# Encoder block on one core: the first tile of x in two transfers, and the root's spread in two rounded passes

## The chip, the cores and the metric

One core of a Trainium2 chip runs the kernel. The metric is the device time of one execution in microseconds (us), taken as the median of several runs. The core has five engines that work side by side: TensorE (PE, matrix products), VectorE (DVE), ScalarE (ACT), GpSimd (POOL) and SyncE (SP, which issues the transfers here). Each runs its own list of instructions in order, and they wait for each other through semaphores.

## The reference

One layer of a bidirectional encoder, batch 1, 1024 tokens, width 1024, all in float32:

```
h = rmsnorm(x, norm1_g)
q, k, v, u = split(h @ w_in)                 # 512, 128, 128, 512 columns
a = attention_mixer(q, k, v, ...)            # 8 query heads, 2 key heads, 2-D rotary positions
p = pool_mixer(u, ...)                       # 4 groups of 128 channels, windows 2/4/8/16
x = x + concat([a, p]) @ w_out
h = rmsnorm(x, norm2_g)
x = x + (silu(h @ w_gate) * (h @ w_up)) @ w_down
```

`rmsnorm` multiplies each token's row by r = 1/sqrt(mean of squares + 1e-6) and by a gain per channel.

## The kernel before

**Products.** Every float32 product is made from rounded (F32R) operands. `split` (L336 to L349) writes an operand's rounded copy, the high half, and then the rest, the low half (`combine`, L351 to L355: source minus high half). Three matmuls, high by high, high by low and low by high (`PASSES`, L324), give one product; matmuls of the feed-forward part are L1176, L1441 and L1494, those of the first projections L490 (k and v), L684 (u) and L601 (q).

**Start.** `load_x` (L434) fetches x in eight tiles of 128 tokens into `qp`; tile 0 goes first, then k's and v's weights (`load_w`, L415, two transfers of 512 KB), then tiles 1 to 7, all on SP's queue. `turn_x` (L458) transposes a tile, eight PE transposes of 128x128 (L474); ACT writes each one's high half (L464) and DVE its low half (L466). `stats_x` (L447) makes r for each token (`rx`, one column for each tile) with an iterated root on DVE (L362 to L373).

**Spread of r.** The u projection is held transposed (channels on partitions), so r, which belongs to a token, has to stand along the free axis, the same on all partitions. `diagonals` (L648) writes for each tile the identity times its column of r (L655, a 128x128 piece of the 1024 wide tile `dgs`); `spread_r` (L660) multiplies a tile of ones by it (L665), which sums each column and so puts r on every partition; ACT copies it out (L669). Two such products with 512 columns each are made, in full float32, just after the first step of the first group of u (`K["spread"]`).

**Who decides the order.** The whole program is written once into a planner, `Flow` (L139): every piece of ACT, DVE and POOL work is a job whose steps have a cost by the functions `act`, `dve`, `pool` and so on (L264 to L286), PE's work advances the planner's clock by the number in `flow.tensor(...)`, transfers by `Flow.load`. Where a step may run on either of two engines (`quicker`, L252, used by `split` and `combine`), the planner takes the one that it expects to end first. The program is rehearsed six times, jobs get ranks from when PE needed them, and the best rehearsal's order is what the engines run. So a changed cost near the start can move low halves between DVE and POOL, and change each engine's order, anywhere behind it. PE's order and SP's are as written.

**Later stages.** After u come the pooling windows (`windows`, L714) with their product (`pool_mix`, L752, matmul L760), the q projection (`q_tile`, L595), attention (L828 scores, L858 transposes of probabilities, L871 values, L908 output), and a feed-forward part of blocks (L1176) and, five times, `down_sums` (L1469), which multiplies sums of operands (steps A11, S1, S2, S4, S3, A12 and A22, each for two operand pairs; L1494) and adds their banks to x by DVE (`into`, L1456). In `down_sums` the two operands of a step are split into a `ring` tile and a `raw` or `wk` tile, high halves by ACT (L340), low halves by DVE or POOL (L355).

Of the kernel before, what the change touches and what calls it, by code (L numbers as in the profile page):

```python
# [10 lines left out]
F32 = mybir.dt.float32  # L11
F32R = mybir.dt.float32r
BF16 = mybir.dt.bfloat16
I32 = mybir.dt.int32
AF = mybir.ActivationFunctionType
ALU = mybir.AluOpType
AX = mybir.AxisListType.X

P = 128
# [14 lines left out]
HALF = S // 2  # L34
# [10 lines left out]
NRAW = 3  # L45
RIM, GAP = 120, 80
K = {
    "pieces": 1, "groups": [[0], [1], [2, 3], [4, 5, 6, 7]], "take": [0, 3], "tables": 2, "spread": [1],
    "ahead": [22, 39], "turn_k": 50, "wq": [60], "mix": [56, 62, 10, 30], "prep_q": [20], "turn_q": [37],
    "wo": [33, 39, 52, 62], "score": [40, 41, 42, 43, 47, 49, 52, 54, 57, 59, 61, 63, 63], "fold": 1,  # L50
    "out": [0, 0, 0, 2, 1, 2, 1, 2], "wo2": [3, 9, 10, 10, 16, 16], "mix_c": 5, "norm": 6, "next_prep": 8,
# [212 lines left out]
def act(n, extra=0.0):  # L264
    return "A", 0.1 + 0.00097 * n + extra


def dve(n):

    return "D", max(0.16, 0.07 + 0.00119 * n)  # L270


def dve_sbuf(n):
    return *dve(n), True
# [15 lines left out]
def block_kernel(  # L290
# [4 lines left out]
    nc = tc.nc  # L295
# [17 lines left out]
    ident = const.tile([P, P], F32, name="ident")  # L313
# [11 lines left out]
    flow = Flow(ranks)  # L325
# [65 lines left out]
    def work(dt=F32, n=D):  # L391
        return wk.tile([P, n], dt, tag="wk", name="wk")
# [50 lines left out]
    rx = const.tile([P, NT], F32, name="rx")  # L443
# [202 lines left out]
    rb, rb_jobs, dg_jobs = [], [], []  # L646

    def diagonals():  # L648
        dgs, ones = work(), work(n=P)
        nc.gpsimd.memset(ones, 1.0)  # L650

        def diagonal(t):
            yield [rx_job[t]]
            yield dve_sbuf(P)
            nc.vector.tensor_scalar(dgs[:, t * P:(t + 1) * P], ident, rx[:, t:t + 1], None, op0=ALU.mult)  # L655

        dg_jobs.extend(flow.add(diagonal(t)) for t in range(NT))
        return dgs, ones

    def spread_r(dgs, ones):  # L660
        rb.append(work())
        for h in range(2):
            pr = bank()
            flow.tensor(0.86, *dg_jobs[4 * h:4 * h + 4])
            nc.tensor.matmul(pr, ones, dgs[:, h * HALF:(h + 1) * HALF], start=True, stop=True)  # L665

            def evacuate(h, pr):
                yield act(HALF)
                nc.scalar.activation(rb[0][:, h * HALF:(h + 1) * HALF], pr, AF.Copy)  # L669

            rb_jobs.append(flow.add(evacuate(h, pr)))
            flow.hold("b1", rb_jobs[-1])
# [850 lines left out]
    groups = K["groups"]  # L1523
# [13 lines left out]
    kf.append(flow.add(k_finish(4, 4)))  # L1537
    pw, pw_job = load_pw()
    dgs, ones = diagonals()
    wq = []  # L1540
    step = 0
# [167 lines left out]
```

## Time and profile before

| | us |
|---|---|
| median of 3 runs | 1088.13 (1088.09 to 1088.22) |
| the profiled execution | 1088.39 |
| its span | 1086.5 |
| PE busy | 1064.8 |
| DVE busy | 738.7 |
| ACT busy | 511.1 |
| POOL busy | 461.9 |

The span runs from the first to the last instruction that the profile shows; 1.89 us of the profiled execution lie outside it. The profiled execution is 0.26 us above the median of the runs. An engine's busy time is what its instructions took, waiting left out. PE is busy for 98% of the span, so the time is the time that its matmuls take, plus the stretches in which it waits.

### The profile page before, as it was taken

To read this page: it belongs to the slowest core of one execution; us is meant where nothing else is said; L and a number is where in the kernel's file an instruction comes from. 1 tells how busy PE (TensorE), PEld (TensorE's weight loads), DVE (VectorE), ACT (ScalarE), POOL (GpSimd) and SP (SyncE) were. 2 spreads that over 40 slices of the span, in tenths; PEclk is the share of its full clock that TensorE was granted. 3 is DMA by queue.
4 is the path that set the end of the run, shared out by engine and by line. 5 is a ranking of instruction groups with operands and counts; after the bars stand their busy time and mean duration, and the time that the engine had idled before them with its cause. 6 is when DMAs were issued, how large, how long until landed. Compare 5 with 4: busy or idle time off the path is not lost.

```text
span 1086.5 us, 13908 instructions
## 1 busy us (share of the span) xinstructions
PE 1064.8 (98%) x5114; PEld 875.4 (81%) x5114; DVE 738.7 (68%) x1214; ACT 511.1 (47%) x904; POOL 461.9 (43%) x367
## 2 busy tenths in 40 slices
PE   7999998999999999999999999999999999999998
PEld 6887876888888888878788887888788878888787
DVE  7888788888676766784964379346944496448745
ACT  6424477666676664633433433433333433343340
POOL 1254344444323223444543465355634463446431
PEclk9999999999999999999999999999999999999999
DMA  7122111000000100130032101220213013110114
GB/s 258 30 78 78 39 41 48 10 21 20 10 21 11 30 30 26 53 110 26 20 97 79 39 20 59 78 78 1 78 59 97 2 39 97 59 40 20 40 58 155
DMA packets 42563, 58.47 MB, mean 54 GB/s; under 512 B 4224, under 2 KB 32768, under 8 KB 42496
## 3 DMA queue, kind: packets, MB, share of 16 engines
q1 hardware_dynamic: 42496, 57.59, 16.5%
q8 instruction: 40, 0.66, 0.3%
q14 instruction: 27, 0.22, 0.1%
HBM read 53.39 MB, written 4.19 MB: 53 GB/s over the span
## 4 chain that ended last, share of the span: by engine, by line
PE 78%; DVE 13%; issue 3%; POOL 3%; ACT 2%; DMA 0%; SPq 0%; ACTq 0%; POOLq 0%; DVEq 0%
PE b L1176 36%; PE b L908 8%; PE b L1494 8%; PE b L871 5%; PE b L828 5%; PE b L858 5%; PE b L684 4%; DVE wk L355 3%; PE b L601 3%; DVE ring L355 2%; PE b L1441 2%; POOL wk L355 2%; DVE qp L1456 2%; PE b L490 2%; DVE nm L837 1%
## 5 line engine op out<-in xcount | busy, mean ns | idle before, releaser
L1176 PE MATMUL b<-wk,ring 128*128 128x512 f32 x1872 | 426.3, 390 | 0.9 <-POOL ring L355 0.7
L1176 PEld LDWEIGHTS b<-wk,ring 128*128 128x128 f32 x1872 | 351.1, 188 | 74.6 <-POOL ring L355 1.1
L340 ACT ACTIVATE ring<-raw 128x512 fp32r<-128x512 f32 x130 | 81.6, 629 | 119.6 <-PE b L1176 57.1
L355 POOL TENSOR_TENSOR ring<-raw,ring 128x512 fp32r<-128x512 f32 x54 | 70.1, 1297 | 157.9 <-ACT ring L340 139.1
L847 POOL TENSOR_SCALAR wk<-wk,rsm 128x1024 f32<-128x1024 f32 x64 | 73.6, 1158 | 132.7 <-ACT wk L839 40.2
L349 DVE TENSOR_TENSOR wk<-b,wk 128x512 fp32r<-128x512 f32 (+1 forms) x160 | 101.7, 658 | 41.4 <-ACT wk L340 40.9
L340 ACT ACTIVATE wk<-b 128x512 fp32r<-128x512 f32 (+1 forms) x160 | 90.3, 576 | 84.0 <-PE b L858 67.1
L1494 PE MATMUL b<-raw,ring 128*128 128x512 f32 x480 | 115.3, 394 | 4.1 <-DVE raw L355 2.5
L1494 PEld LDWEIGHTS b<-raw,ring 128*128 128x128 f32 x480 | 88.6, 188 | 29.2 <-DVE qp L1456 5.9
L355 DVE TENSOR_TENSOR ring<-raw,ring 128x512 fp32r<-128x512 f32 x76 | 57.8, 761 | 76.9 <-ACT ring L340 76.9
L1456 DVE TENSOR_TENSOR qp<-qp,b 128x512 f32<-128x512 f32 (+1 forms) x157 | 101.8, 674 | 9.0 <-PE b L1441 8.9
L908 PE MATMUL b<-wk 128*128 128x512 f32 x384 | 102.5, 397 | 0.0
L355 POOL TENSOR_TENSOR wk<-wk 128x512 f32<-128x512 f32 (+3 forms) x52 | 75.9, 1467 | 35.0 <-ACT wk L340 25.8
L828 PE MATMUL b<-kT,wk 128*128 128x512 f32 x256 | 89.5, 431 | 0.5 <-ACT wk L804 0.5
L871 PE MATMUL b<-wk,vv 128*128 128x512 f32 x256 | 83.1, 400 | 4.3 <-DVE wk L349 4.2
L1494 PE MATMUL b<-wk,ring 128*128 128x512 f32 x360 | 85.0, 392 | 0.2
L837 DVE TENSOR_REDUCE nm<-b 128x1 f32<-128x1024 f32 x64 | 77.9, 1217 | 9.1 <-PE b L828 7.9
L908 PEld LDWEIGHTS b<-wk 128*128 128x128 f32 x384 | 70.7, 188 | 14.9
L355 POOL TENSOR_TENSOR ring<-silu,ring 128x512 fp32r<-128x512 f32 x35 | 53.9, 1540 | 63.4 <-ACT ring L340 63.4
L1494 PEld LDWEIGHTS b<-wk,ring 128*128 128x128 f32 x360 | 67.2, 188 | 16.4 <-DVE ring L355 1.8
L858 PEld LDWEIGHTS b<-ident,wk 128*128 128x128 f32 x512 | 63.6, 140 | 16.9 <-POOL wk L847 0.5
L858 PE MATMUL b<-ident,wk 128*128 128x128 f32 x512 | 76.7, 272 | 0.3 <-POOL wk L847 0.3
(142 smaller groups left out, 1454.1 us busy)
## 6 DMA issues: line engine op xcount, KB each, us to landing
raw<-in_w_gate_dram SPq DMA_DIRECT2D x22, 512.0 KB, 3.7
raw<-in_w_up_dram SPq DMA_DIRECT2D x22, 512.0 KB, 3.8
wk<-in_w_down_dram SPq DMA_DIRECT2D x20, 512.0 KB, 4.7
raw<-in_w_in_dram SPq DMA_DIRECT2D x10, 512.0 KB, 4.2
qp<-in_x_dram SPq DMA_DIRECT2D x8, 512.0 KB, 8.2
raw<-in_w_out_dram SPq DMA_DIRECT2D x8, 512.0 KB, 3.4
out_dram<-qp SPq DMA_DIRECT2D x15, 256.0 KB, 2.0
raw<-in_x_dram SPq DMA_DIRECT2D x14, 256.0 KB, 2.7
```

What stands on the lines that cost most here:

```text
L340: nc.scalar.activation(hi, src, AF.Copy)
L349: nc.vector.tensor_tensor(lo, src, hi.bitcast(F32), op=ALU.subtract)
L355: (nc.gpsimd if way[0] == "G" else nc.vector).tensor_tensor(dst, a, b, op=op)
L828: nc.tensor.matmul(s[:, c * 512:(c + 1) * 512], qT[t][0][:, h * P:(h + 1) * P], kT[:, kv, b, c * 512:(c + 1) * 512], start=(b == 0), stop= ...
L837: nc.vector.tensor_reduce(nm, s, axis=AX, op=ALU.max, negate=True)
L847: nc.gpsimd.tensor_scalar(pe, pe, rs, 1.0, op0=ALU.mult, op1=ALU.mult)
L858: nc.tensor.transpose(pt[:, j * P:(j + 1) * P], pe[:, c * P:(c + 1) * P], ident)
L871: nc.tensor.matmul(po[t, kv], vt, ps[:, b], start=(c == 0 and b == 0), stop=(c == NT - 1 and b == 1))
L908: nc.tensor.matmul(self.py, mix[self.t][a][:, k, :], wo[k][b][:, self.cs], start=(self.i == 0 and i == 0), stop=(self.i == NK - 1 and i == 2))
L1176: nc.tensor.matmul(bank_, w[0][:, a, i], x[:, b], start=(start and i == 0 and j == 0), stop=(stop and i == PARTS - 1 and j == 2), skip_gro ...
L1456: nc.vector.tensor_tensor(dst, dst, src, op=op)
L1494: nc.tensor.matmul(banks[t][0], x[:, a, t * P:(t + 1) * P], y[:, b], start=(own == name and i == 0 and j == 0), stop=(i == 1 and j == 2), ...
```

## The change

`K["pieces"]` goes from 1 to 2: tile 0 of x (512 KB) is fetched as two transfers of 128x512 (256 KB each), so that its first four transposes need the first one only; the other tiles are fetched as before. The spread of r gets its diagonals as rounded pairs: ACT writes the high half (identity times r, rounded), DVE the rest, and each 512-column product is made of two F32R matmuls that add up in the bank, in place of a full float32 one. `ones` is written by POOL from the identity in place of a memset, and one more work tile is held.

```diff
 K = {
-    "pieces": 1, "groups": [[0], [1], [2, 3], [4, 5, 6, 7]], "take": [0, 3], "tables": 2, "spread": [1],
+    "pieces": 2, "groups": [[0], [1], [2, 3], [4, 5, 6, 7]], "take": [0, 3], "tables": 2, "spread": [1],
@@
     def diagonals():
-        dgs, ones = work(), work(n=P)
-        nc.gpsimd.memset(ones, 1.0)
+        dgs, ones = [work(F32R) for _ in range(2)], work(F32R, n=P)
+        nc.gpsimd.tensor_scalar(ones, ident, 0.0, 1.0, op0=ALU.mult, op1=ALU.add)
 
         def diagonal(t):
+            c = slice(t * P, (t + 1) * P)
             yield [rx_job[t]]
+            yield act(P)
+            nc.scalar.activation(dgs[0][:, c], ident, AF.Copy, scale=rx[:, t:t + 1])
             yield dve_sbuf(P)
-            nc.vector.tensor_scalar(dgs[:, t * P:(t + 1) * P], ident, rx[:, t:t + 1], None, op0=ALU.mult)
+            nc.vector.scalar_tensor_tensor(dgs[1][:, c], ident, rx[:, t:t + 1], dgs[0][:, c].bitcast(F32), op0=ALU.mult, op1=ALU.subtract)
@@
-            flow.tensor(0.86, *dg_jobs[4 * h:4 * h + 4])
-            nc.tensor.matmul(pr, ones, dgs[:, h * HALF:(h + 1) * HALF], start=True, stop=True)
+            flow.tensor(0.462, *dg_jobs[4 * h:4 * h + 4])
+            for i in range(2):
+                nc.tensor.matmul(pr, ones, dgs[i][:, h * HALF:(h + 1) * HALF], start=(i == 0), stop=(i == 1))
```

Lines behind the change stand 4 further down in the changed kernel (L1456 becomes L1460).

**What moves.** PE's list differs only in the spread, SP's only in the first tile of x. The lists of DVE, POOL and ACT come out of the planner anew, and differ in many places. Three are shown; a name with a number is one tile, and numbers differ between the kernels throughout.

POOL, low halves during the windows and the q weights, before:

```order
L355 TENSOR_TENSOR wk_1053<-wk_945,wk_1052 128x1024
L355 TENSOR_TENSOR wk_1089<-raw_1086,wk_1088 128x1024
L704 MEMSET le_1118 128x8
L706 COPY le_1118<-wk_951 128x16
L711 TENSOR_TENSOR le_1119<-le_1118 128x23
L355 TENSOR_TENSOR wk_1163<-wk_959,wk_1162 128x1024
```

and of the change:

```order
L355 TENSOR_TENSOR wk_1063<-wk_895,wk_1062 128x1024
L355 TENSOR_TENSOR wk_1103<-raw_1100,wk_1102 128x1024
L355 TENSOR_TENSOR wk_1107<-raw_1104,wk_1106 128x1024
L708 MEMSET le_1134 128x8
L710 COPY le_1134<-wk_965 128x16
L715 TENSOR_TENSOR le_1135<-le_1134 128x23
```

The rows that read a `raw` tile are low halves of q's weights, the third and, now, the fourth transfer of them too. The last row of before, the low half of the pooled values of the third group (source wk_959), is no longer POOL's: DVE makes it, in place of the low half of the fourth transfer.

DVE, in the first `down_sums`, around its step S3, before:

```order
L355 TENSOR_TENSOR wk_4986<-wk_4986 128x512
L355 TENSOR_TENSOR ring_5363<-wk_4535,ring_5363 128x512
L355 TENSOR_TENSOR ring_5384<-silu_4611,ring_5384 128x512
L1456 TENSOR_TENSOR qp_84<-qp_84,b1_5255 128x512
L1456 TENSOR_TENSOR qp_84<-qp_84,b3_5260 128x512
L355 TENSOR_TENSOR silu_4980<-silu_4981,silu_4982 128x512
L1456 TENSOR_TENSOR qp_84<-qp_84,b3_5266 128x512
L355 TENSOR_TENSOR wk_5031<-wk_5031 128x512
L1456 TENSOR_TENSOR qp_84<-qp_84,b3_5273 128x512
L355 TENSOR_TENSOR ring_5426<-silu_4646,ring_5426 128x512
L355 TENSOR_TENSOR raw_5406<-wk_5031,raw_5406 128x512
L355 TENSOR_TENSOR wk_5427<-wk_4988,wk_5427 128x512
```

and of the change:

```order
L355 TENSOR_TENSOR ring_5374<-wk_4547,ring_5374 128x512
L355 TENSOR_TENSOR wk_4999<-wk_4999 128x512
L355 TENSOR_TENSOR ring_5395<-silu_4623,ring_5395 128x512
L1460 TENSOR_TENSOR qp_84<-qp_84,b1_5267 128x512
L1460 TENSOR_TENSOR qp_84<-qp_84,b1_5272 128x512
L355 TENSOR_TENSOR silu_4993<-silu_4994,silu_4995 128x512
L1460 TENSOR_TENSOR qp_84<-qp_84,b1_5278 128x512
L355 TENSOR_TENSOR wk_5041<-wk_5041 128x512
L1460 TENSOR_TENSOR qp_84<-qp_84,b3_5285 128x512
L355 TENSOR_TENSOR raw_5416<-wk_5041,raw_5416 128x512
L355 TENSOR_TENSOR ring_5437<-silu_4658,ring_5437 128x512
L355 TENSOR_TENSOR wk_5438<-wk_5001,wk_5438 128x512
```

Two things changed places: the weight sum (wk_4986, now wk_4999) goes from before the two `ring` low halves to between them, and the `raw` low half goes ahead of the `ring` one behind the four `into` additions. The same stands in all five `down_sums`.

DVE at the start (L466: low halves of tile 0's transposes, 128x128; L342 and L355: halves of k's and v's weights), before:

```order
L466 SCALAR_TENSOR_TENSOR wk_114<-b2_150,pk_72,wk_106 128x128
L342 CAST wk_130<-raw_128 128x256
L466 SCALAR_TENSOR_TENSOR wk_114<-b1_147,pk_72,wk_106 128x128
L342 CAST wk_130<-raw_128 128x256
L355 TENSOR_TENSOR wk_131<-raw_128,wk_130 128x256
```

and of the change:

```order
L466 SCALAR_TENSOR_TENSOR wk_114<-b2_151,pk_72,wk_106 128x128
L466 SCALAR_TENSOR_TENSOR wk_114<-b1_148,pk_72,wk_106 128x128
L466 SCALAR_TENSOR_TENSOR wk_115<-b1_154,pk_72,wk_107 128x128
L342 CAST wk_131<-raw_129 128x256 x2
L466 SCALAR_TENSOR_TENSOR wk_115<-b2_161,pk_72,wk_107 128x128
```

Two more of tile 0's low halves stand ahead of the first copy of the weights.

## Rows read from the trace of the kernel before

**Rows 1.** The page, part 1: busy us (share of the span) xinstructions.

```profile
PE 1064.8 (98%) x5114; PEld 875.4 (81%) x5114; DVE 738.7 (68%) x1214; ACT 511.1 (47%) x904; POOL 461.9 (43%) x367
```

**Rows 2.** Busy time by stretch: us, then PE, PEld, DVE, ACT, POOL busy, PEclk, DMA share, GB/s.

```profile
105.00:250.00 145.00, 139.61 (x730) 112.96 (x729) 116.03 (x212) 95.29 (x162) 65.79 (x53) 1.00 0.09 30
250.00:1086.00 836.00, 828.16 (x3846) 679.75 (x3843) 535.23 (x783) 367.34 (x644) 360.42 (x270) 1.00 0.16 50
```

**Rows 3.** Chain of work that ended last, the start: start us, us, what.

```profile
1.16 3.88 DMA qp<-in_x_dram
...
7.05 0.20 DVE wk L342
...
8.87 0.52 DVE wk L466 x2
```

**Rows 4.** Timeline of SP and PE, the start: start us, us, engine, line, operation [idle before <-releaser].

```profile
1.16 0.42 SPq L438 DMA_DIRECT2D qp<-in_x_dram  x1
...
9.32 0.98 PE L490 MATMUL b<-wk 128*128 128x256 f32 x3
...
12.54 0.60 PE L490 MATMUL b<-wk 128*128 128x256 f32 x3
```

**Rows 5.** Chain of work that ended last, 41 to 46 us.

```profile
41.69 1.39 PE b L684 x6
43.07 1.72 PE b L665 x4
```

**Rows 6.** Timeline of DVE, the diagonals.

```profile
40.22 0.86 DVE L655 TENSOR_SCALAR wk<-ident,rx 128x128 f32<-128x128 f32 x4
42.44 0.35 DVE L504 SCALAR_TENSOR_TENSOR vv<-b,rx,vv 128x128 fp32r<-128x128 f32 x1 [1.36 <-ACT vv L502]
```

**Rows 7.** Timelines of POOL, DVE and PE, 25 to 30 us.

```profile
25.39 2.37 POOL L355 TENSOR_TENSOR wk<-raw,wk 128x1024 fp32r<-128x1024 f32 x1 [11.61 <-DVE ra L364]
...
25.96 1.83 DVE L366 TENSOR_SCALAR rx<-ra 128x2 int32<-128x2 int32 x1
...
29.71 4.54 PE L490 MATMUL b<-wk 128*128 128x256 f32 x34 [0.20 <-DVE wk L466]
```

**Rows 8.** Timelines of PE, ACT, DVE and POOL, the q weights.

```profile
97.51 3.47 PE L601 MATMUL b<-wk 128*128 128x512 f32 x14 [0.40 <-DVE wk L355]
...
102.25 1.43 PE L760 MATMUL b<-wk 128*128 128x512 f32 x5 [1.04 <-POOL wk L355]
...
94.18 1.06 ACT L340 ACTIVATE wk<-raw 128x1024 fp32r<-128x1024 f32 x1 [3.44 <-DMA raw<-in_w_in_dram]
...
96.21 1.25 DVE L355 TENSOR_TENSOR wk<-raw,wk 128x1024 fp32r<-128x1024 f32 x1
...
90.82 3.14 POOL L355 TENSOR_TENSOR wk<-raw,wk 128x1024 fp32r<-128x1024 f32 x1 [2.46 <-ACT wk L340]
...
99.82 2.37 POOL L355 TENSOR_TENSOR wk<-wk 128x1024 fp32r<-128x1024 f32 x1 [3.44 <-ACT wk L340]
```

**Rows 9.** Timelines of PE, DVE and POOL, first `down_sums`.

```profile
542.38 1.19 PE L1494 MATMUL b<-raw,ring 128*128 128x512 f32 x4 [0.24 <-DVE qp L1456]
544.08 2.83 PE L1494 MATMUL b<-raw,ring 128*128 128x512 f32 x11 [0.51 <-DVE raw L355]
...
534.52 0.81 DVE L355 TENSOR_TENSOR wk<-wk 128x512 f32<-128x512 f32 x1
...
536.96 1.77 DVE L355 TENSOR_TENSOR ring<-silu,ring 128x512 fp32r<-128x512 f32 x1
...
542.25 1.17 DVE L355 TENSOR_TENSOR ring<-silu,ring 128x512 fp32r<-128x512 f32 x1
543.34 0.68 DVE L355 TENSOR_TENSOR raw<-wk,raw 128x512 fp32r<-128x512 f32 x1
...
536.57 1.61 POOL L355 TENSOR_TENSOR raw<-wk,raw 128x512 fp32r<-128x512 f32 x1
```

**Rows 10.** The page, part 6: DMA issues, KB each, us to landing.

```profile
raw<-in_x_dram SPq DMA_DIRECT2D x14, 256.0 KB, 2.7
```

## The prediction

> **What bounds the kernel now.** I read the page first: PE is busy for 98% of the span [rows 1], so time comes out only where its matmuls get shorter or where it waits. Next the busy time by stretch: from 250 us on PE is idle for 836.00 − 828.16 = 7.84 us, between 105 and 250 us for 5.39 us [rows 2], at a granted clock of 1.00. That idle time, and what little there is before 105 us, is all that a better order can win. Then the chain of waits where the change stands: the start hangs on the landing of tile 0, after it on DVE [rows 3], and the spread lies on the chain as PE work [rows 5]. Last the timelines, at the places where the new order moves something that PE waits for [rows 7 to 9].
>
> **The spread of r.** The full float32 products take 1.72 us on the chain; six F32R matmuls of the same 128x512 shape, next to them, take 1.39 us, 0.232 each [rows 5]. Four of those replace them: 0.93 us. PE has no wait there, so this is −0.8 us.
>
> It holds if the pairs are ready. DVE finished the old diagonals at 40.22 + 0.86 = 41.08 us, 2.0 us before the first product at 43.07, and was idle for 1.36 us before 42.44 [rows 5, 6]. The eight DVE steps change form: 128x128 with two tensors read, of which the 0.35 us row is the nearest, against 0.86 / 4 = 0.22 in the row now [rows 6]; that is about 1 us more on DVE, in part covered by its idle time. The eight new ACT steps must come before them, ACT's price for 128x128 being unseen for this operation. From what stands ahead of them I put the last pair at 41.5 to 42.0 us, 0.5 us or more before PE. Cost: nothing; if the cover is gone, PE waits up to 0.9 us, which undoes the gain. The POOL write of `ones`, long before, has no reader waiting: nothing.
>
> **The first tile.** Tile 0 is issued at 1.16 us and lands 3.88 us later, and PE starts on it [rows 3]. Its first half is half of the bytes; I put it at 4.0 us, about 1.1 us earlier, the second half about where the whole was. That frees PE's first transposes, ACT's and DVE's halves. But the extra issue, 0.42 us [rows 4], makes all transfers behind it on SP's queue that much later: both weight transfers and seven tiles. The first weight copy on DVE is at 7.05 us [rows 3], set by order as much as by data, and from there DVE is almost without a gap up to 14.7 us, where PE takes over the chain. What counts is how much of DVE's work is done before the weights come: the new order puts two more low halves there, 0.26 each [rows 3]: −0.5 us. Bounds: −1.1, if everything moves with the first half, and +0.5, if the chain moves with the later transfers. PE's work here runs slow for its form: three matmuls of 256 columns take 0.98 us at 9.32 and 0.60 at 12.54 [rows 4]; work brought forward in this stretch is worth less on PE than its length, which is why I stay well inside −1.1. I take −0.5.
>
> At 25 to 30 us a POOL low half of 2.37 us stood beside a DVE step of two elements that took 1.83 us, and PE waited 0.20 at the end of it [rows 7]. The new order gives POOL two plain copies first and DVE a 1024 wide low half; of this a 1.2 us step on DVE may land on the same chain. Between −0.4 (this wait and its like before it) and +1.2, I take −0.2, since PE's rows show next to no idle time to win or cover here.
>
> **The q weights.** PE waited 0.40 us for DVE's low half of the fourth weight transfer and 1.04 us for POOL's low half of pooled values [rows 8]. They change engines. The pooled half takes about 1.25 us on DVE in place of 2.37 and DVE is freed of the 1.25 us before it, so the 1.04 goes. The weight's half can start on POOL when ACT is done, at 94.18 + 1.06 = 95.24 us, and takes 2.37 to 3.14 us [rows 8]: done at 97.6 to 98.4 in place of 97.46, so the 0.40 grows by 0.2 to 0.9 us. Sum −0.8 to −0.1: I take −0.4. Attention behind it also gets another order on DVE and POOL; of its 5.39 us of idle time [rows 2] some may go and some come: 0, bounds −1.5 and +1.5.
>
> **The five down_sums.** In each PE waits twice, 0.24 us for an addition and 0.51 for the `raw` low half at 543.34, which stands behind a `ring` low half of 1.17 us [rows 9]; the pair recurs five times alike. Now the `raw` half goes first, and the 0.51 goes, even with the additions later, since PE is then later by as much. But the weight sum, 0.81 us alone, moves behind the first `ring` half, where POOL's work up to 536.57 + 1.61 = 538.18 us stretches two-input DVE steps (1.77 for the `ring` half, against 0.68 for such a step alone) [rows 9]. The additions that PE waits for start after both. From 536.96 the two take 0.81 to 1.77 and 0.68 to 1.17, to 538.45 to 539.90, where the `ring` half alone ended at 538.73: between −0.3 and +1.2, I take +0.35, near the middle, for POOL ends within it. Net −0.15 each, −0.75 in all; bounds 5 × (−0.3 − 0.51), about −4, limited by the recorded idle to 5 × −0.75, and 5 × (1.2 − 0.51) = +3.5.
>
> Which half is slowed by POOL bears on this. DVE's 1.17 us came beside POOL work and its 0.68 after it; by the Trainium skill, GPSIMD Engine Reference, Specifications, the two engines share interfaces to SBUF, and DVE instructions with two SBUF inputs contend. The trace agrees for the low halves, while a DVE step with one small input took 1.83 us beside POOL [rows 7], which that rule alone would not give. By the rule the `raw` half, now beside the POOL step, would take 1.17 itself, and still end before PE needs it.
>
> **Sum.** −0.8 − 0.5 − 0.2 − 0.4 − 0.75 = −2.65 us on the profiled execution's 1088.39, so 1085.74; that execution lies 0.26 above the median of the runs, so I predict **1085.5**.
>
> **The rivals.** *The new order gives nothing.* The additions come 0.5 us later, which eats the `raw` gain, and the q weights break even; the spread, the start and the stage behind it remain: −1.5, or 1086.6. For it: order changes where PE is 98% busy have little to win. Chance 0.25.
>
> *An early gain is eaten by the q weights or attention.* POOL's half ends at its late end and DVE's new steps stand before something that PE needs: +0.9 there and +1 in attention on top of the first rival's −1.5, about 1088.3 − 0.2 = 1088.1. For it: the 1.04 us wait shows how late POOL's halves come. Against: the pooled half leaves POOL. Chance 0.12.
>
> *Slower: the weight sum beside POOL.* If the weight sum and the `ring` half behind it both take 1.77 us, the additions start 536.96 + 3.54 − 538.73 = 1.77 us later, a net 1.26 in each of five: +6.3 against −1.9 of the rest: 1092.5. It decides for slower than before once the additions are 0.51 + 1.9 / 5 = 0.9 us late. For it: one step did take 1.77 us there. Against: POOL's busy stretch ends 1.2 us into the pair, so both can't be stretched in full by the same POOL work. Chance 0.08, with 1090 as its milder form.
>
> *The split does not do what it says.* The second half pays a transfer's fixed time after the first: 256 KB took 2.7 us [rows 10], so it would land near 6.7 us, ACT's last four copies wait for it, and the start gives nothing: 1086.0. Chance 0.05. The Trainium skill, DMA: Bandwidth & Descriptors, Bandwidth, speaks against small transfers (batch to 1 MiB or more); by that the two halves cost more than the whole and the start gives nothing, as in this rival. The trace has 2.7 us for 256 KB [rows 10] and 3.88 for the 512 KB of tile 0 [rows 3], so two halves one after the other would be slower, as the page has it, and no row shows two at once.
>
> **How the numbers follow.** The forecast has 0.50; its own range is 1084 to 1086.8. No change that a measurement can tell is within 0.2%, 2.2 us: 1085.95 to 1090.31. Of the forecast case some 0.38 lies below 1085.95; of the first rival and the split 0.08, and attention's lower bound adds a little to both: faster 0.50. Slower is the weight-sum rival in its strong form and part of the second: 0.08. The rest, 0.42, is no change. The range is 1082.8 (the start and the `raw` gain in full) to 1088.8 (the early gain eaten, the additions late).
>
> **What would show it.** Right: PE's spread at 0.9 us with no wait before it; first transposes near 4.1 us, and PE about 0.5 us ahead at 12 us; the 102.25 wait gone; in each `down_sums` no wait for a `raw` half, and one for an addition of about 0.6 us. Wrong: a wait for the diagonals, PE not ahead at 30 us, a wait over 1.3 us for the q weights, or waits of over a microsecond for the additions.

## The result: 5.5 us faster, from the order of five later stages

| | before | after |
|---|---|---|
| median of 6 runs each | 1088.18 us (1088.09 to 1088.59) | 1082.69 us (1081.47 to 1083.05) |
| profiled execution | 1088.39 us | 1083.04 us |
| its span | 1086.5 us | 1081.0 us |

The ratio is 0.9947, interval 0.9936 to 0.9958. I predicted 1085.5 us in a range of 1082.8 to 1088.8: the direction held, the gain that I forecast (2.7 us) was half of the one measured, and the median lies 0.1 us below the range.

The profile after, page part 1 (answers to [rows 1]):

```profile
PE 1061.1 (98%) x5114; PEld 876.2 (81%) x5114; DVE 742.1 (69%) x1210; ACT 513.6 (48%) x912; POOL 459.0 (42%) x371
```

PE's busy time fell by 3.7 us with as many matmuls, though the spread explains 0.8 only. The busy time by stretch of after, same columns as [rows 2]:

```profile
105.00:250.00 145.00, 140.00 (x730) 112.99 (x729) 112.70 (x212) 94.80 (x162) 64.90 (x51) 1.00 0.09 30
250.00:1081.00 831.00, 825.53 (x3848) 680.29 (x3846) 541.91 (x783) 368.36 (x646) 356.53 (x271) 1.00 0.16 51
```

Attention's idle time hardly moved (5.00 us for 5.39). From 250 us on the idle time is 5.47 us for 7.84, and the rest of the gain lies inside what counts as busy.

**Where the time went.** PE runs the same list in both kernels but for the spread, so one can subtract the start of each matmul before from its start after, in the two profiled executions (one of each kernel). The difference, read at the stages' borders:

| stage | predicted | measured |
|---|---|---|
| start, to 24.6 us | −0.5 | +1.87 |
| 25 to 33 us | −0.2 | +0.36 |
| spread of r | −0.8 | −0.80 |
| q weights | −0.4 | −0.79 |
| attention | 0 | −0.25 |
| feed-forward up to the first `down_sums` | 0 | +0.96 |
| five `down_sums` | 5 × −0.15 | −6.82 (5 × −1.36) |
| sum | −2.65 | −5.47 |

The start (timelines of PE and DVE, after; answers to [rows 3] and [rows 4]):

```profile
4.35 1.30 PE L474 MATMUL b<-ident,qp 128*128 128x128 f32 x5 [4.35 <-DMA qp<-in_x_dram]
...
8.49 0.55 PE L490 MATMUL b<-wk 128*128 128x256 f32 x1 [1.69 <-DVE wk L342]
...
10.66 0.48 PE L474 MATMUL b<-ident,qp 128*128 128x128 f32 x1 [0.66 <-DMA qp<-in_x_dram]
...
8.05 0.49 DVE L342 CAST wk<-raw 128x256 fp32r<-128x256 f32 x2 [1.31 <-DMA raw<-in_w_in_dram]
```

The first transposes start 0.83 us earlier than before (5.18), as meant. But DVE then stands 1.31 us for the weights and copies them first at 8.05, a microsecond later than the 7.05 of before, and PE waits for the second tile of x too. How long the transfers took, the first half of tile 0 and k's and v's second weight transfer in after (line, queue, KB, us from issue to landing; they are issued at 1.16 and 2.6 us):

```profile
qp<-in_x_dram SPq DMA_DIRECT2D x1, 256.0 KB, 3.0
...
raw<-in_w_in_dram SPq DMA_DIRECT2D x1, 512.0 KB, 6.8
```

and the same weight transfer before, issued at 2.1 us:

```profile
raw<-in_w_in_dram SPq DMA_DIRECT2D x1, 512.0 KB, 5.7
```

Issued 0.48 us later, it also took 1.1 us longer: it landed about 1.6 us later. The first weight transfer, on which DVE's copy at 8.05 waits, was as much later: it took 5.9 us for 4.8, and was issued 0.48 us later too.

From 25 us (PE, DVE, POOL, after; answers to [rows 7]):

```profile
29.09 0.66 PE L474 MATMUL b<-ident,qp 128*128 128x128 f32 x4 [1.28 <-DVE wk L466]
...
24.12 2.00 DVE L355 TENSOR_TENSOR wk<-raw,wk 128x1024 fp32r<-128x1024 f32 x1
...
26.31 2.07 DVE L362 TENSOR_SCALAR ms<-ssq 128x2 f32<-128x2 f32 x1
...
25.14 3.21 POOL L355 TENSOR_TENSOR wk<-raw,wk 128x1024 fp32r<-128x1024 f32 x1
```

This is the bound of +1.2 us that I gave and did not take: DVE's 1024 wide low half and a step of two elements were both held beside POOL, and PE waited 1.28 us for them, of which the later stretch to 33 us gave some back.

The spread (chain of work, then DVE, after; answers to [rows 5] and [rows 6]):

```profile
43.93 1.39 PE b L688 x6
45.31 0.91 PE b L669 x4
...
42.42 0.87 DVE L658 SCALAR_TENSOR_TENSOR wk<-ident,rx,wk 128x128 fp32r<-128x128 f32 x3
...
43.63 1.18 DVE L658 SCALAR_TENSOR_TENSOR wk<-ident,rx,wk 128x128 fp32r<-128x128 f32 x4
```

0.91 us for 1.72, and no wait. The pairs came 0.5 us ahead of the first product, as I had said, in a stretch that is itself 2 us late.

The q weights (PE, POOL, DVE, after; answers to [rows 8]):

```profile
99.34 3.47 PE L601 MATMUL b<-wk 128*128 128x512 f32 x14 [0.85 <-POOL wk L355]
102.65 1.52 PE L764 MATMUL b<-wk 128*128 128x512 f32 x6
...
96.92 2.37 POOL L355 TENSOR_TENSOR wk<-raw,wk 128x1024 fp32r<-128x1024 f32 x1 [1.58 <-ACT wk L340]
...
100.81 1.22 DVE L355 TENSOR_TENSOR wk<-wk 128x1024 fp32r<-128x1024 f32 x1
```

The 1.04 us wait is gone and the 0.40 has become 0.85, as foretold.

In the feed-forward part one new wait stands out, for a low half that POOL now makes (PE, after):

```profile
482.96 1.20 PE L1180 MATMUL b<-wk,ring 128*128 128x512 f32 x4 [0.62 <-POOL ring L355]
```

The first `down_sums`, PE, DVE, POOL and ACT of after (answers to [rows 9]):

```profile
534.95 5.63 PE L1498 MATMUL b<-wk,ring 128*128 128x512 f32 x24
540.42 2.29 PE L1498 MATMUL b<-raw,ring 128*128 128x512 f32 x9
542.92 3.90 PE L1498 MATMUL b<-raw,ring 128*128 128x512 f32 x15 [0.22 <-DVE qp L1460]
...
536.77 1.11 DVE L355 TENSOR_TENSOR ring<-wk,ring 128x512 fp32r<-128x512 f32 x1 [0.28 <-ACT ring L340]
537.80 0.68 DVE L355 TENSOR_TENSOR wk<-wk 128x512 f32<-128x512 f32 x1
538.41 0.68 DVE L355 TENSOR_TENSOR ring<-silu,ring 128x512 fp32r<-128x512 f32 x1
539.01 1.27 DVE L1460 TENSOR_TENSOR qp<-qp,b 128x512 f32<-128x512 f32 x2
...
542.97 1.00 DVE L355 TENSOR_TENSOR raw<-wk,raw 128x512 fp32r<-128x512 f32 x1
...
536.03 1.30 POOL L355 TENSOR_TENSOR wk<-wk 128x512 fp32r<-128x512 f32 x1
539.23 1.30 POOL L355 TENSOR_TENSOR raw<-wk,raw 128x512 fp32r<-128x512 f32 x1 [1.89 <-ACT raw L340]
...
538.52 0.63 ACT L340 ACTIVATE raw<-wk 128x512 fp32r<-128x512 f32 x1 [1.26 <-DVE wk L355]
```

and what stood there before, beside the rows already shown (PE, DVE, POOL):

```profile
533.64 6.01 PE L1494 MATMUL b<-wk,ring 128*128 128x512 f32 x24
539.49 2.65 PE L1494 MATMUL b<-raw,ring 128*128 128x512 f32 x9
...
535.48 1.55 DVE L355 TENSOR_TENSOR ring<-wk,ring 128x512 fp32r<-128x512 f32 x1 [0.15 <-ACT ring L340]
...
534.74 1.75 POOL L355 TENSOR_TENSOR wk<-wk 128x512 fp32r<-128x512 f32 x1
```

Before, POOL's two steps (534.74 to 538.18) lay on DVE's two `ring` halves, and each stretched the other: 1.55 and 1.77 us on DVE, 1.75 and 1.61 on POOL. After, POOL's first step ends at 537.33 and its second starts at 539.23, since that second one is the low half of the weight sum, whose high half ACT makes from DVE's sum (ACT waits 1.26 us for it), and the sum now comes later. In POOL's pause DVE's sum and second `ring` half take 0.68 each, and POOL's steps 1.30 each. PE gains in three places: the same 24 matmuls take 5.63 for 6.01, the same nine 2.29 for 2.65, and the wait of 0.51 for the `raw` half is gone. By PE's starts these are 0.32, 0.36 and 0.73: the 1.4 us of the stage (the last includes about 0.1 from the waits for the additions). The first two are not in PE's rows, where they sit inside busy matmuls, but the rows of PE's weight loads (PEld, the same stretch of before) name them:

```profile
536.54 0.19 PEld L1494 LDWEIGHTS b<-wk,ring 128*128 128x128 f32 x1 [0.22 <-POOL wk L355]
537.09 2.14 PEld L1494 LDWEIGHTS b<-wk,ring 128*128 128x128 f32 x10 [0.36 <-DVE ring L355]
...
541.18 0.53 PEld L1494 LDWEIGHTS b<-raw,ring 128*128 128x128 f32 x3 [0.53 <-DVE qp L1456]
```

A weight load waits for POOL's first step, one for DVE's stretched `ring` half, and one for an addition to x.

### The profile page after: what moved, and what is told of

Its sections match the earlier page's. It is cut to its first block, busy times and chain, and to the rows that moved or that the text cites. A ratio compares the mean times of both kernels' runs of the same rounds, so it can differ in the third digit from the quotient of the medians.

```text
span 1081.0 us, 13923 instructions
## 1 busy us (share of the span) xinstructions
PE 1061.1 (98%) x5114; PEld 876.2 (81%) x5114; DVE 742.1 (69%) x1210; ACT 513.6 (48%) x912; POOL 459.0 (42%) x371
## 4 chain that ended last, share of the span: by engine, by line
PE 79%; DVE 10%; issue 3%; POOL 3%; ACT 3%; DMA 1%; SPq 0%; POOLq 0%; ACTq 0%; DVEq 0%
PE b L1180 36%; PE b L912 8%; PE b L1498 8%; PE b L875 5%; PE b L832 5%; PE b L862 4%; PE b L688 4%; PE b L601 3%; DVE wk L355 3%; POOL wk L355 2%; PE b L1445 2%; DVE qp L1460 2%; PE b L490 2%; DVE ring L355 1%; DVE nm L841 1%
## 5 line engine op out<-in xcount | busy, mean ns | idle before, releaser
L355 POOL TENSOR_TENSOR ring<-raw,ring 128x512 fp32r<-128x512 f32 x49 | 63.3, 1292 | 149.5 <-ACT ring L340 136.0
L355 DVE TENSOR_TENSOR ring<-raw,ring 128x512 fp32r<-128x512 f32 x81 | 63.7, 789 | 72.2 <-ACT ring L340 71.7
L1460 DVE TENSOR_TENSOR qp<-qp,b 128x512 f32<-128x512 f32 (+1 forms) x157 | 100.5, 673 | 9.0 <-PE b L1445 8.9
L355 POOL TENSOR_TENSOR wk<-wk 128x512 fp32r<-128x512 f32 (+3 forms) x51 | 71.5, 1409 | 43.5 <-ACT wk L340 20.3
L843 ACT ACTIVATE wk<-b,nm 128x1024 f32<-128x1024 f32 x64 | 71.4, 1116 | 10.4 <-DVE nm L841 9.5
```

Source lines behind the costliest of these rows:

```text
L355: (nc.gpsimd if way[0] == "G" else nc.vector).tensor_tensor(dst, a, b, op=op)
L1460: nc.vector.tensor_tensor(dst, dst, src, op=op)
```

## The experiments

Three theories stood against each other: the gain is in the order of `down_sums` alone; the start or the spread carries part of it; and, within `down_sums`, which of the exchanged places does it. Some kernels take the orders of the changed kernel and undo a part. Others replay the orders of before: the planner's last order is noted as one list of steps for each engine, a line moves one step in it, and the engines run the edited lists.

### Taking the split or the spread away

One transfer for tile 0, all orders as in the changed kernel:

```diff
-                nc.sync.dma_start(qp[:, t, i * n:(i + 1) * n], x2d[t * P:(t + 1) * P, i * n:(i + 1) * n])
+                if i == 0:
+                    nc.sync.dma_start(qp[:, t, :], x2d[t * P:(t + 1) * P, :])
```

> The changed kernel with every engine's order kept, only that tile 0 of x comes in one transfer again. Theory: the split made the weights and tile 1 land late (weights waited for until 8.05 us, tile 1 until 10.6, against 6.4 and 9.05 before), so the first weights are back near 6.5 us and PE is about 2 us earlier at 30 us: about 1080.7 us (1080.0 to 1081.6). Rival, lateness by chance of that one profiled execution: 1082.3 to 1083.2, the first transposes 0.8 us later again. Second rival, the new order itself makes the start late (the 1.28 us wait at 29 us stays): about 1081.8.

Measured: 1081.19 us (1081.01 to 1081.53), ratio 0.9931 [0.9916, 0.9945]. Without the split the changed kernel is 1.5 us faster in the medians, and 1.8 when each is set against the runs of before beside it: the split costs time. PE's wait for DVE, near 27 us here, stays at 0.70 us, and is 0.96, 1.26 and 0.80 in three more kernels below with one transfer and orders of this kind. So that wait belongs to the order and not to the split, as the second rival had it.

The kernel before, its orders kept, with tile 0 in two transfers:

```diff
-                nc.sync.dma_start(qp[:, t, i * n:(i + 1) * n], x2d[t * P:(t + 1) * P, i * n:(i + 1) * n])
+                for j in range(2 if t == 0 else 1):
+                    m = D // 2 if t == 0 else D
+                    nc.sync.dma_start(qp[:, t, j * m:(j + 1) * m], x2d[t * P:(t + 1) * P, j * m:(j + 1) * m])
```

> The kernel before with every engine's order kept, only that tile 0 of x comes in two transfers. Theory: the transfers behind the split land 1 to 1.5 us later, and what of it reaches PE at 30 us makes it 0.7 to 1.6 us slower: about 1089.3 us. Rival, the first half's 0.8 us is worth something and the rest was chance: 1087.4 to 1088.1.

Measured: 1089.63 us (1088.38 to 1090.47, 10 runs) beside 1088.46 for before, ratio 1.0008 [0.9999, 1.0018]: 1.2 us slower in the medians, with nine of the ten runs above the median of before, but an interval that still includes no change. The run above, where the split is taken away, points the same way.

The kernel before, its orders kept, with the new spread. Its diff is that of `diagonals` and `spread_r` above without the two lines that tell the planner, so that the plan stays as it was:

```diff
-            yield act(P)
...
-            flow.tensor(0.462, *dg_jobs[4 * h:4 * h + 4])
+            flow.tensor(0.86, *dg_jobs[4 * h:4 * h + 4])
```

> The kernel before with its orders kept, only that the spread is made from rounded pairs (eight ACT steps put in at the places where DVE made the diagonals). Theory: four matmuls of 0.23 us for 1.72 us, ready in time: 1087.35 us (1087.1 to 1087.6). Rival, PE waits for the pairs: 1088.0 to 1088.6 and a wait at 43 us.

Measured: 1087.62 us (1087.36 to 1087.81), ratio 0.9991 [0.9981, 1.0]: −0.8 us, and no run of the two overlaps.

The changed kernel's orders with neither: one transfer, and the float32 product of `ones` and diagonals (the ACT copies are still made, and not read):

```diff
-            nc.vector.scalar_tensor_tensor(dgs[1][:, c], ident, rx[:, t:t + 1], dgs[0][:, c].bitcast(F32), op0=ALU.mult, op1=ALU.subtract)
+            nc.vector.tensor_scalar(dgs[1][:, c], ident, rx[:, t:t + 1], None, op0=ALU.mult)
...
-            for i in range(2):
-                nc.tensor.matmul(pr, ones, dgs[i][:, h * HALF:(h + 1) * HALF], start=(i == 0), stop=(i == 1))
+            nc.tensor.matmul(pr, ones, dgs[1][:, h * HALF:(h + 1) * HALF], start=True, stop=True)
```

> The changed kernel's orders with the old full float32 product and with one transfer (ACT's eight copies are still made, and not read): what the new order alone does. Theory, the new order is the whole of the gain (about 6.8 us in the five down_sums, 1.2 at the q weights) and the two edits by themselves are worth -0.8 and about +2: 1081.5 us (1080.8 to 1082.4). Rival, the gain in the down_sums hangs on the later start and not on the order: over 1085.

Measured: 1082.16 us (1081.79 to 1082.92), ratio 0.994 [0.9925, 0.9955]. The order alone is worth 6.3 us. The split gives 1.2 to 1.5 of it back, the spread adds 0.8 to 1.0.

### Where the order came from

The new spread alone, planned anew: the whole change but for one number.

```diff
-    "pieces": 2, "groups": [[0], [1], [2, 3], [4, 5, 6, 7]], "take": [0, 3], "tables": 2, "spread": [1],
+    "pieces": 1, "groups": [[0], [1], [2, 3], [4, 5, 6, 7]], "take": [0, 3], "tables": 2, "spread": [1],
```

> The change's new spread alone, planned by the planner itself (tile 0 in one transfer in the plan too). The planner leaves the down_sums as they were before. Theory: then the gain there is not had and only the spread's 0.8 us is, with a little from the q weights either way: 1087.3 us (1086.3 to 1088.0). Rival, the gain comes from the spread's side of the change: below 1085.

Measured: 1087.83 us (1087.46 to 1089.64), ratio 0.9996 [0.9987, 1.0006]. And that number alone, 2 in place of 1 in the kernel before, planned anew:

> The change's two transfers alone, planned by the planner itself (old spread). The down_sums stay as before here too. Theory: slower than before by the late transfers, 1089.3 us (1088.3 to 1090.3). Rival, the planner's new start order pays for the late transfers: 1087.5 to 1088.2.

Measured: 1093.24 us (1092.98 to 1093.64), ratio 1.0045 [1.003, 1.006], slower by 4.8 and 3 us beyond the end of what I expected. In both, `down_sums` has the order of before. So neither edit brings the gain: only together did they tip the planner, some 500 us ahead of the stages that gained. That the planner's choice has no tie to either edit is argued from this, not shown further.

The 4.8 us of the second are more than the split. PE's timeline at its q weights, then its busy time by stretch (columns of [rows 2]), in the one profiled execution:

```profile
100.51 5.07 PE L601 MATMUL b<-wk 128*128 128x512 f32 x14 [1.86 <-POOL wk L355]
...
99.00:102.00 3.00, 1.49 (x4) 1.25 (x5) 2.96 (x4) 0.00 (x0) 1.86 (x4) 0.82 0.38 115
102.00:105.00 3.00, 3.00 (x10) 2.29 (x9) 1.32 (x2) 2.12 (x3) 0.54 (x1) 0.61 0.37 145
```

PE waited 1.86 us for POOL's half, and the granted clock was 0.82 and then 0.61 in the two stretches shown, so part of them was run at the 1.2 GHz level: the 14 matmuls that take 3.47 us in the changed kernel took 5.07. Wait and slower matmuls are 3.5 us, where before PE waited 0.40: some 3.1 us more. The rest is the late start: by PE's starts this kernel is 1.5 us late ahead of its q weights and 4.6 behind them.

### Which exchange in `down_sums`

On the changed kernel with one transfer, the weight sum goes back ahead of S4's first `ring` half:

```diff
+        if final and name == "S4" and p % 2 == 1:
+            gen_l = held_back(gen_l, made_pair[p - 1]["T3"], 2)
```

> The kernel of x1 (changed orders, one transfer), only that in each down_sums the weight sum of step S3 goes back ahead of the ring low half of step S4, as before the change. Theory: POOL's low half of that sum then runs again beside DVE's two ring low halves, which go back from about 1.1 and 0.7 us to 1.5 and 1.8, and the additions that PE waits for are late by 0.5 to 0.7 us in each of five: 1081.2 + 2.5 to 3.5, about 1084.2 us, with PE's wait for an addition near 0.7 us. Rival, the place of the raw low half alone makes the gain: 1081 to 1081.8.

Measured: 1080.5 us (1079.94 to 1080.7), ratio 0.9926 [0.991, 0.9943]. This is 0.7 us faster than with one transfer alone, and no run of the two overlaps: my theory that the gain hangs on the sum's place behind the `ring` half fell.

On the same kernel, the `raw` low half goes back behind the `ring` one of A12, each in wait of the other's place:

```diff
+        if final and name == "S3" and p % 2 == 1:
+            gen_r = opens(held_back(gen_r, mark_of(p - 1, "A12")), mark_of(p - 1, "S3"), lambda: made["split T3"])
+        if final and name == "A12" and p % 2 == 0:
+            gen_r = held_back(gen_r, mark_of(p, "S3"))
```

> The kernel of x1, only that in each down_sums the raw low half of step S3 goes back behind the ring low half of step A12. Theory: PE waits for it again, 0.5 to 0.7 us in each of five, 1081.2 + 2.5 to 3.5: about 1084.2 us, and the wait is put down to a raw low half. Rival, with DVE ahead it comes in time anyway and the weight sum alone makes the gain: 1081 to 1081.8.

Measured: 1084.82 us (1083.84 to 1085.78), ratio 0.9967 [0.9954, 0.998]: 3.6 us lost, 0.7 in each stage, and the wait is back in PE's timeline:

```profile
542.44 2.81 PE L1523 MATMUL b<-raw,ring 128*128 128x512 f32 x11 [0.51 <-DVE raw L355]
```

Then from the other side, on the replayed orders of before. The `raw` low half ahead of A12's `ring` half, alone:

```diff
+        move((at["y", b, "S3"], 1), (at["x", a, "A12"], 1), 0)
```

> The kernel before with every list of every engine replayed, only that in each of the five down_sums DVE makes the raw low half of S3 ahead of the ring low half of A12. Theory: PE's wait for the raw half goes, 0.5 to 0.7 us in each of five: 1088.3 - 2.5 to 3.6, about 1085.3 us. Rival, another operand or an addition is late in its place: 1087.5 to 1088.5.

Measured: 1085.34 us (1085.0 to 1086.09), ratio 0.9972 [0.9962, 0.9983]: −3.0 us. One more place where the orders differ, which the prediction left out: one of S1's two additions to x, on DVE, goes from before S4's first `ring` half to behind it, so that it stands right ahead of the weight sum.

```diff
+        move((at["add", b, "S1", 1], 0), (at["x", a, "S4"], 2), 1)
```

> The kernel before replayed, only that in each down_sums the second addition of S1 on DVE stands behind the ring low half of S4's first pair in place of ahead of it. Theory: the addition, which POOL's work does not slow, then fills the stretch in which POOL works, and the weight sum and the two ring low halves behind it come when POOL is idle (0.7 us each in place of 1.55 and 1.77): S4's operand and S2's additions are earlier by 0.3 to 0.7 us in each of five: about 1085.3 us (1084.3 to 1086.6). Rival, three additions in a row make the same halves later: 1088.5 to 1091. Second rival, the place of one addition is worth nothing, and the engines of the low halves of S1 and S2 are the cause: 1087.8 to 1088.6.

Measured: 1083.81 us (1083.54 to 1084.0), ratio 0.9957 [0.9942, 0.9972]: −4.5 us, beyond the range of the theory and the largest single part. DVE and POOL there, and PE's wait that stays:

```profile
535.01 1.47 DVE L377 TENSOR_TENSOR wk<-wk 128x512 f32<-128x512 f32 x1
536.40 0.68 DVE L377 TENSOR_TENSOR ring<-wk,ring 128x512 fp32r<-128x512 f32 x1
537.00 0.68 DVE L377 TENSOR_TENSOR ring<-silu,ring 128x512 fp32r<-128x512 f32 x1
...
534.63 1.30 POOL L377 TENSOR_TENSOR wk<-wk 128x512 fp32r<-128x512 f32 x1
537.22 1.62 POOL L377 TENSOR_TENSOR raw<-wk,raw 128x512 fp32r<-128x512 f32 x1 [1.29 <-ACT raw L362]
...
543.04 2.79 PE L1518 MATMUL b<-raw,ring 128*128 128x512 f32 x11 [0.40 <-DVE raw L377]
```

The addition ahead makes the weight sum 0.5 us later (535.01 for 534.52). POOL's first step then lies on that sum alone, and its second waits for the sum's high half. The first `ring` half falls into the pause, and the second lies beside POOL's second step for its last 0.46 us only: 0.68 each, where before they took 1.55 and 1.77. The sum itself takes 1.47 here, and POOL's second step still 1.62.

The low halves of the second operand pair in S1 and S2 change engines, DVE for POOL and POOL for DVE, alone:

```diff
+        for name in ("S1", "S2"):
+            x, y = (at["x", b, name], 1), (at["y", b, name], 1)
+            i, j = lists["G"].index(x), lists["D"].index(y)
+            lists["G"][i], lists["D"][j] = y, x
```

> The kernel before replayed, only that in each down_sums the two low halves of the second pair of S1, and those of S2, exchange engines (the ring half from POOL to DVE, the raw half from DVE to POOL). Theory: nothing of it is waited for: 1087.9 to 1088.9 us. Rival, this is what makes S4's operand and the additions earlier: 1084 to 1086. Second rival, the raw halves come late from POOL, as feared: over 1090.

Measured: 1086.9 us (1086.6 to 1088.07), ratio 0.9987 [0.9977, 0.9996]: −1.4 us, between the two theories. All three edits on the orders of before:

> The kernel before replayed, with the three exchanges of the last runs together in each down_sums, the weight sum left ahead. Theory: they add up to what the trace shows of the whole change there, 1.4 us in each of five: 1088.3 - 7 = 1081.3 us (1080.6 to 1082.4), with nothing of the rest of the change in it. Rival, the gain needs the weight sum's new place too: over 1083.5.

Measured: 1080.7 us (1080.3 to 1080.94), ratio 0.9928 [0.9914, 0.9943]: −7.6 us, with nothing of the change itself. The parts add up to 9.0, so they overlap by 1.3. PE no longer waits at all in the stage's two halves, and neither do its weight loads:

```profile
533.97 5.60 PE L1518 MATMUL b<-wk,ring 128*128 128x512 f32 x24
539.41 5.60 PE L1518 MATMUL b<-raw,ring 128*128 128x512 f32 x24
```

### The q weights and the start

On the orders of before, the low halves of q's fourth weight transfer and of the third group's pooled values change engines:

```diff
+    lists["D"].remove(item)
+    lists["G"].insert(lists["G"].index((at["wq", 2], 1)) + 1, item)
+    lists["G"].remove(low)
+    lists["D"].insert(max(n for n, i in enumerate(lists["D"]) if i[0] == y) + 3, low)
```

> The kernel before replayed, only that the low half of q's fourth weight transfer goes from DVE to POOL and that of the pooled values of the third group from POOL to DVE. Theory: the 1.04 us wait goes and the 0.40 us one grows by 0.2 to 0.9: 1087.4 to 1088.1, about 1087.6 us. Rival, the gain there came from something else in the changed order: 1088.2 to 1089, with a wait over 1.2 us for q's weights.

Measured: 1088.28 us (1088.09 to 1088.67), ratio 0.9998 [0.9988, 1.0007]. No change that can be told, as the rival had it: the 1.04 wait is gone, and the other one has grown to 1.47, by 1.07 where the theory had 0.2 to 0.9. POOL's half took 2.98 us here, from 95.57, with DVE's step of 1.22 us at 95.11 beside it; in the changed kernel that DVE step ends at 96.42, before POOL starts at 96.92, and POOL's half takes 2.37.

Is it the split, or any transfer more on SP's queue? The constants, issued first, in two parts, the last 4 KB behind tile 0:

```diff
-    nc.sync.dma_start(pk, packed)
+    cut = NCONST - 2 * NG
+    nc.sync.dma_start(pk[:, 0:cut], packed[:, 0:cut])
...
+    nc.sync.dma_start(pk[:, cut:NCONST], packed[:, cut:NCONST])
```

> The kernel before, its constants fetched in two parts, of which the second (4 KB) is issued behind tile 0: one more issue at the place where the split has one, and tile 0 whole. Theory, the issue alone makes the transfers behind late: both weights 0.45 us later and no more, 1088.4 to 1088.8 us. Rival, any transfer more ahead of the weights makes them 1.5 us late: 1089.3 us or over. Second rival, an issue more is not felt: 1088.0 to 1088.4.

Measured: 1089.6 us (1088.38 to 1090.39), ratio 1.0007 [0.9998, 1.0016]: 1.1 us slower in the medians, nine of ten runs above the median of before, and again an interval that includes no change. PE waits for the second tile of x, which is 1.4 us late, as are k's and v's second weights; the first weights land only 0.5 us late, about the added issue, and are copied on time:

```profile
10.56 0.45 PE L474 MATMUL b<-ident,qp 128*128 128x128 f32 x1 [1.72 <-DMA qp<-in_x_dram]
```

That 4 KB are too few to be the load, and that it is one transfer more as such, is argued and not shown. How often the later ones come late varies: in the profiled execution of the run with exchanged engines, without any additional transfer, the second weights came 0.8 us late and the second tile's first transpose started at 10.00 us, and that execution was the second slowest of its ten. So part of what one profiled execution shows can be chance.

Last, the second half of tile 0 issued behind both weight transfers:

```diff
+                m = D // 2 if t == 0 else D
+                nc.sync.dma_start(qp[:, t, 0:m], x2d[t * P:(t + 1) * P, 0:m])
...
+    nc.sync.dma_start(qp[:, 0, D // 2:D], x2d[0:P, D // 2:D])
```

> The kernel before with tile 0 in two transfers, the second half issued behind both weight transfers. If the weights were late because the second half stood ahead of them, the first weight copy on DVE can start at about 6.5 us or earlier; PE's last four transposes then wait for the half until about 7.5 us. If two smaller transfers as such slow what follows, the weights are late still, near 8 us. The time is not the question here: 1088 to 1091 us.

Measured: 1089.33 us (1089.07 to 1089.91), ratio 1.0007 [0.9997, 1.0018]. PE starts at 4.13, but its fifth transpose comes later than the weights did before:

```profile
8.65 1.11 PE L475 MATMUL b<-ident,qp 128*128 128x128 f32 x4 [3.43 <-DMA qp<-in_x_dram]
```

The weights are on time here: DVE copies the first at 6.41 us, after 0.40 of waiting, and not at 8.05:

```profile
6.41 0.29 DVE L342 CAST wk<-raw 128x256 fp32r<-128x256 f32 x1 [0.40 <-DMA raw<-in_w_in_dram]
```

Tile 0 comes in two parts here too, so what comes late is what stands behind the added transfer, and not every transfer of the queue.

### The parts that pay, together

The orders of before with the three exchanges in `down_sums`, that of the q weights, and the new spread; tile 0 in one transfer:

> The kernel before replayed, with the three exchanges in each down_sums, the exchange at the q weights and the new spread; tile 0 in one transfer. Theory: the parts add up, 1080.7 (the three exchanges) - 0.8 (spread) - 0.6 (q weights) = 1079.3 us (1078.6 to 1080.2), faster than the changed kernel by about 3.4. Rival, the start or attention takes some of it back: 1080.2 to 1081.5.

Measured: 1079.61 us (1079.38 to 1079.67), ratio 0.9915 [0.99, 0.993]. It beats the kernel before by 8.9 us and the changed kernel by 3.1. Its page, part 1:

```profile
PE 1059.2 (98%) x5114; PEld 877.5 (81%) x5114; DVE 737.4 (68%) x1214; ACT 514.0 (48%) x912; POOL 454.8 (42%) x367
```

DVE and POOL are busy for 1.3 and 7.1 us less than before with as many instructions; the rows above, with the same steps at 1.30 and 0.68 us that took up to 1.75 and 1.77, fit contention no longer paid. That this is all of it is argued, not shown.

## Why the prediction was right and where it was wrong

**The spread: right.** −0.8 foretold, −0.8 measured alone and in place. The cover was thinner than I put it: in the run with the spread alone DVE's last pairs end at 43.5 us, where I had the last at 41.5 to 42.0. The second product starts then, so nothing was lost.

**The first tile: wrong in sign**, +1.87 for −0.5, outside my upper bound of +0.5. Two steps failed.
- The extra issue "makes all transfers behind it on SP's queue that much later", by its 0.42 us. They came some 1.6 us later. I had also read DVE's first weight copy at 7.05 us as "set by order as much as by data"; with the data later it became a wait of 1.31 us. With the orders of before, the split alone makes PE's matmul at 24.6 us start 1.17 us late.
- "The new order puts two more low halves there [...]: −0.5 us". In the four kernels with one transfer and the changed kernel's orders, whole or but for one exchange, the same matmul is 0.35 to 0.79 us late, not early: DVE makes the two halves first and copies the weights after them. In the kernel with the `raw` half behind again, DVE's timeline has that copy at 7.32 us, and at 6.97 in the kernel before.

The rival in which the second half pays a fixed time after the first fell as well: by the transfers' times it landed at 1.63 + 3.2 = 4.8 us, no later than the whole tile did. Two at once took 3.0 and 3.2 us, where [rows 10] have 2.7 for one. The Trainium skill, DMA: Bandwidth & Descriptors, Bandwidth, says to batch transfers to 1 MiB or more. The trace doesn't have the two halves cost more themselves, and has those behind them pay.

**25 to 33 us: the range's upper bound came**, +1.2 for one wait, and was partly made good. The wait is the order's: 0.70 to 1.26 us in the four kernels with one transfer. I had named the step and then put −0.2, because PE had little idle time to lose there; that is no reason against a loss.

**The q weights: right where they stood**, one wait for another, but by themselves worth nothing that can be told (−0.2 in the medians). The changed kernel is 0.8 us better there, since POOL's half took 2.37 us and not 2.98: DVE's step ahead of it, whose place I didn't price, is what differs in the rows.

**The five `down_sums`: right in sign, wrong ninefold in size**, −0.15 for −1.36 each, and this is where the prediction as a whole went wrong. Two steps failed.
- "POOL's work up to 536.57 + 1.61 = 538.18 us" I left where it was. But POOL's second step is the low half of the weight sum, the very thing that the order moves: make the sum later, and POOL pauses. I then charged the additions +0.35 for being later; PE waits 0.22 for them in place of 0.24, where my sign of being right was 0.6. The price of 0.81 us for the sum "alone" was a reading beside POOL's step from 534.74; alone it is 0.68. The moved addition of S1, which the experiments show to be the largest part (−0.9 each), I didn't see, nor the exchanged engines.
- "Limited by the recorded idle to 5 × −0.75". The stage gave 1.4, since two of the three gains were waits inside busy rows of PE. They could be read before, in the rows of its weight loads (0.22, 0.36 and 0.53 us, shown above) and in the matmuls: 24 in 6.01 us are 0.250 each, where the six next to the spread take 0.232 [rows 5], so 0.4 us were missing. Without that limit my own bound of −0.3 − 0.51 for each stage was still too small, since the additions' part of it left POOL's work in its place. The range's low end didn't even hold that bound: with −3.75 here and −1.1 at the start the terms would have reached 1081.9 us, and would have held the median with the start wrong in sign, which would have been luck.

By the Trainium skill, GPSIMD Engine Reference, Specifications, POOL contends with DVE instructions that have two SBUF inputs or run in a 2-port mode. The runs agree for the low halves (0.68 alone, up to 1.77 beside POOL), and for the additions, which have one SBUF input: the two took 1.27 us beside POOL's step at 539.23 and 1.27 before, with POOL idle. The step of two elements has one input and was held for 2.07 us at 26.31; no run shows in which mode it ran, so it speaks neither for nor against the rule. I cited the half of the rule on two inputs, and priced one side of it: that POOL's step, too, gets shorter when DVE's are not beside it, I left out.

**The rivals.** That the new order gives nothing, and that an early gain is eaten, both fell with `down_sums`, though the early loss was there. The slower one (the weight sum and the `ring` half both held beside POOL) has the first half right, in part: 1.11 us for the first `ring` half, and 0.68 for the sum, because POOL went away. The sum of the rival with the early gain eaten is 1088.5 us by its own terms (−1.5 + 0.9 + 1), where I wrote 1088.1.

## What to carry to other kernels

When an order moves a step, follow its result to the engine that reads it: here one addition moved by a place made POOL pause, and the pause, not the step, gave the time. PE's recorded idle time isn't the limit of a gain: read the rows of its weight loads beside it, and compare busy rows of the same matmuls with the best row of their form. And when a planner decides the order, an edit's effect is what the edit does plus what the planner makes of it: measure them apart, for here the first was worth +0.4 us or so (the split's loss against the spread's gain) and the second −6.

## What the hardware showed that I had not expected

- A transfer added ahead of others on one queue made those behind it late by more than the 0.47 us from one issue to the next. In the profiled executions, 256 KB made both weight transfers about 1.6 us late; 4 KB made the first weights 0.5 and the second weights and second tile 1.4 us late. The kernel's medians rose by 1.2 and 1.1 us, each with an interval that includes no change, and one execution without an added transfer had such a lateness, of 0.8 us.
- After a PE wait of 1.86 us the granted clock was 0.82 and 0.61 in two stretches of 3 us, part of them thus at the 1.2 GHz level, and the next 14 matmuls took 1.6 us more; after the waits of 1.04 and 1.47 us in the same stage of other kernels it stayed at 1.00. That is one execution of each.
- POOL's 128x512 low half takes 1.30 us alone and 1.5 to 1.75 beside DVE's: the contention costs both sides.
